# First mixture of a two-block transformer: experts taken by token count, 64 places for the three smallest, general path moved

## The chip, the cores and the metric

The kernel is one program on 1 core of one Trainium2 chip. The metric is the time of one execution on the device in microseconds (us). The three runs of the kernel before took 2213.13, 2216.81 and 2223.36 us, median 2216.81.

## The reference

A network of two blocks, 256 tokens of width 1024, all in float32. The part that matters here is the first mixture of experts, in the middle of the program:

```python
def moe_swiglu(h, router_w, router_b, w13, w2):
    logits = (h @ router_w).astype(jnp.float32) + router_b.astype(jnp.float32)
    top_val, top_idx = lax.top_k(logits, TOP_K_EXPERTS)
    top_w = jax.nn.softmax(top_val, axis=-1)
    gates = jnp.sum(jax.nn.one_hot(top_idx, N_EXPERTS, dtype=jnp.float32) * top_w[..., None], axis=-2)
    y = jnp.zeros_like(h)
    for e in range(N_EXPERTS):
        y = y + gates[..., e:e + 1] * swiglu(h, w13[e], w2[e])
    return y

def swiglu(h, w13, w2):
    a, b = jnp.split(h @ w13, 2, axis=-1)
    return (jax.nn.silu(a) * b) @ w2
```

`w13[e]` is 1024x7168 and `w2[e]` 3584x1024, so an expert has 44.04 MB of weights and all eight 352.3 MB. Only the tokens that chose an expert count for it. With the inputs of the reference the eight experts get 56, 70, 46, 49, 50, 90, 67 and 84 of the 512 choices.

## The kernel before

**Places.** An expert computes on CAP1 = 96 places: `select` makes a 0/1 matrix `q` (token by place), `fetch` brings the expert's tokens to the columns of `x` with matmuls, two experts at a time, `back` turns `q` round into `qT`, and `finish` adds the weighted results to the residual `R` with it. If one expert has more than 96 tokens, `overflow` (the general path, under a `tc.If` on a count that every engine loads into a register) does the rest; it stands ahead of the first `select`.

**Matmuls.** The weights move through the PE array; the tokens are the loaded side. A piece is 128 rows by 1024 columns of weights, 0.524 MB, and an expert has 84 of them, 56 of `w13` and 28 of `w2`. `unit` (L1212) splits the 96 places into three column groups of 32 that run side by side, each over three quarters of the piece's columns, 512 and then 256; a fourth group of 32 array columns takes the last quarter of the columns for all three. In total nine matmuls a piece; a float32 matmul shows as two records, so a piece shows as 18.

**Loop.** 33 steps `i`: step `i` does chunk `j = i % 4` of `w13` of expert `e = i // 4` (`first`), then the chunk of `w2` that belongs to step `i-1` (`down`), then `turn` transposes. Four steps make a position: position `e` runs expert `e`. At the last step `weighted`, `finish(7)` and `post(tb)` (residual and the two norms, for each half tb of the tokens) lead into block 2, whose first matmuls need `w_in`.

**Stream.** All weights of the program come through one list of loads, issued on SP's queue in program order by `Stream._load` (L136), each when the tile that it takes is free: a tile is free when PE has read it last. In the mixture the buffers are 9 `raw` tiles of 1 MB, `rh`/`rl` (1 MB) and, up to the mark `spl1` near the end, five pairs `wh`/`wl` (5 MB): 15 MB. Behind the mixture's weights the same list goes on with `w_in` of block 2, whose tiles are split into a high and a low part, `wh` on ACT (L149) and `wl` on DVE or, for the pieces named in `BEHIND`, on POOL (L153):

```python
        pool = (j, i) in self.pool
        after = self.behind if pool else self.after
        with self.k.tc.issue_after(after) if after is not None else ExitStack():
            (nc.gpsimd if pool else nc.vector).tensor_tensor(l, src, h.bitcast(F32), op=OP.subtract)
```

`FEW` limits how many of these splits may be made ahead of the end of the mixture.

Of the kernel before, what the change touches and what calls it, by code (L numbers as in the profile page):

```python
# [34 lines left out]
RAW2 = 7  # L35
FEW = 2
NB = 3
URGENT = 3000
TAIL = 2
CAP1 = 96  # L40
WIDE = (1024, 1024, 1024, 512)
# [5 lines left out]
HELD = 1  # L47
BEHIND = ((-1, 4), (0, 4))
POW = (1, 3, 5)
# [26 lines left out]
class Stream:  # L76


    def __init__(self, k, specs):
        self.k, self.specs = k, specs  # L80
        self.raw, self.sp = {}, {}
        self.pools = []
        self.cur = -1
        self.low = -1
        self.nd = 0

        self.pieces = []
        for j, (_, nk, n) in enumerate(specs):
            if nk:
                c = 2 if nk * n > 1024 else 1  # L90
                self.pieces += [(j, i, c) for i in range(c)]
        self.done = {}
        self.after = None
        self.hold = False
        self.limit = None
        self.behind = None
        self.pool = ()
        self.np = 0
        self.first = 0

# [23 lines left out]
    def _load(self, most=10 ** 6):  # L124
        while self.nd < min(len(self.specs), most):
            p = self._place(self.nd)
            if p is None:
                return
            j = self.nd
            m = len(p[4])  # L130
            ts = [p[0].tile([128, 2048 // m], F32, name=x) for x in p[4]]
            p[2].append(j)
            for view, src in self.specs[j][0]:
                nk = src.shape[1] // m
                for i, t in enumerate(ts):
                    self.k.nc.sync.dma_start(view(t, nk), src[:, nk * i:nk * i + nk])  # L136
            self.raw[j] = ts[0] if m == 1 else ts
            self.nd += 1
# [76 lines left out]
class K:  # L215
# [251 lines left out]
    def plan(self):  # L467
# [76 lines left out]
        ada(a1, 5, 1)  # L544
        self.marks["attn"] = len(sp)
        for i in range(33):
            if i < 32:
                e, j = divmod(i, 4)
                if i == 30:
                    self.marks["spl1"] = len(sp)  # L550
                nk = 2048 // WIDE[j]
                for kh in range(8 // nk):
                    for o in range(2):
                        sp.append(wspec(A["moe_w13"][0, e], 128 * nk * kh, nk, 3584 * o + 1024 * j, WIDE[j], False))
            if i:
                e, j = divmod(i - 1, 4)
                for kh in range(WIDE[j] // 256):
                    sp.append(wspec(A["moe_w2"][0, e], 1024 * j + 256 * kh, 2, 0, 1024, False))
        self.marks["moe"] = len(sp)
# [41 lines left out]

        self.S.pool = [(self.marks[x] + i // 2, i % 2) for x, n in zip(("moe", "moe2"), BEHIND) for i in range(*n)]
        self.S.add(self.raw, NB)

# [473 lines left out]

    def ranks(self, sel, n, bank, pos, mx):

# [7 lines left out]
        for tb in range(2):  # L1088
            nc.vector.scalar_tensor_tensor(pos[:, tb], ps[:, n * tb:n * tb + n], 1.0, sel[:, tb], op0=OP.add, op1=OP.mult)
            nc.vector.tensor_scalar(pos[:, tb], pos[:, tb], -1.0, None, op0=OP.add)  # L1090
        nc.vector.tensor_reduce(mx, ps[:, 2 * n:3 * n], axis=AX.X, op=OP.max)

# [28 lines left out]
    def moe_in(self, mp, rp, R):  # L1121

        nc, A, keep = self.nc, self.A, self.keep
        self.route_consts(mp, CAP1, 128, mp.tile([128, 2, 192], F32, name="q", bufs=1)[:, 0, 0:128])
        rw = mp.tile([128, 8, 8], F32, name="rw", bufs=1)
# [43 lines left out]
    def moe(self, mp, R, T, post):  # L1169
# [4 lines left out]
        mx = sm.tile([128, 1], F32, name="mx")  # L1174
        self.ranks(sel, 8, 7, pos, mx)
        w13 = A["moe_w13"][0]

        def select(p):

            q = mp.tile([128, 2, 192], F32R, name="q", bufs=1)  # L1180
            for i in range(2):
                for tb in range(2):
                    nc.vector.tensor_scalar(q[:, tb, 96 * i:96 * i + 96], self.slots[:, 0:96], pos[:, tb, 2 * p + i:2 * p + i + 1], None, op0=OP.is_equal)
            return q

        def fetch(q, x, k):

            ps = self.bank(7)
            for j in range(2):
                for i, (src, tb) in enumerate((src, tb) for src in (nh, nl) for tb in range(2)):  # L1190
                    self.mm(ps[:, 192 * j:192 * j + 192], src[:, tb, 128 * (k + j):128 * (k + j) + 128], q[:, tb], i == 0, i == 3)
            nc.scalar.activation(x[:, k:k + 2], ps[:, 0:384].rearrange("p (k n) -> p k n", k=2), AF.Copy)

# [11 lines left out]

        def room():
            a, b = tokens(), mp.tile([128, 768], F32, name="hT", bufs=1)
            a = a.rearrange("p k n -> p (k n)")
            return [a[:, 256 * k:256 * k + 256] for k in range(6)] + [b[:, 256 * k:256 * k + 256] for k in range(2)]

        self.overflow(mp, room, ("th", "tl"),
                      R, nh, nl, None, None, pos, gate, mx, self.G2, CAP1, 8, 3584,  # L1212
                      w13[:, :, 0:3584], w13[:, :, 3584:7168], A["moe_w2"][0], "o (k p) n -> p (o k) n")
        q = select(0)
        x = tokens()
        for k in range(0, 8, 2):
            fetch(q, x, k)

        y = None

        def unit(out, lhs, rhs, wide, first, last, shared=(True, True)):
# [5 lines left out]
            for c in range(0, 3 * n, m):  # L1227
# [4 lines left out]
                for r in range(c // n, (c + w) // n):  # L1232
                    self.mm(out(3, n * r, n), lhs(r, True), rhs[:, 3 * n:4 * n], start and n * r == c, stop and n * (r + 1) == c + w)

        def first(x, wide):
# [26 lines left out]

        def turn(h, wide):

            nb = 3 * wide // 512
            hT = mp.tile([128, 768], F32, name="hT", bufs=1)
# [27 lines left out]
        def weighted(e):  # L1294

            ys = []
            for h in range(2):
                yg = sm.tile([128, 512], F32, name="t512", bufs=3)
                n = 256 if h else 512
                nc.vector.tensor_tensor(yg[0:96, 0:n], y[h][0:96, 0:n], self.G2[0:96, 512 * h:512 * h + n], op=OP.mult)  # L1300
                if h:
                    for g in range(3):
                        t, c = (y[0], 256 * g) if g < 2 else (y[1], 0)
                        nc.vector.tensor_tensor(yg[32 * g:32 * g + 32, 256:512], t[96:128, c:c + 256], self.G2[96:128, 768:1024], op=OP.mult)
                if e < 7:
                    yh = mp.tile([128, 512], F32R, name="th")[0:96]
                    yl = mp.tile([128, 512], F32R, name="tl")[0:96]
                    self.split(yh, yl, yg[0:96])
                    ys.append((yh, yl))
                else:  # L1310
                    ys.append((yg[0:96],))
            return ys

        def finish(e, qT, ys):
            after = None
            for tb in range(2):
                pc = [self.bank(5 + h) for h in range(2)]
                for h in range(2):
                    for i, part in enumerate(ys[h]):
                        self.mm(pc[h], qT[:, tb] if e < 7 else qT[:, tb].bitcast(F32), part, i == 0, i == len(ys[h]) - 1)  # L1320
                with self.tc.issue_after(after) if after is not None else ExitStack():
                    for h in range(2):
                        c = slice(512 * h, 512 * h + 512)
                        nc.vector.scalar_tensor_tensor(R[:, tb, c], pc[h], gate[:, tb, e:e + 1], R[:, tb, c], op0=OP.mult, op1=OP.add)
                if e == 7:
# [4 lines left out]
        for i in range(33):  # L1330
            e, j = divmod(i, 4)
            if i < 32:
# [5 lines left out]
                if j == 0:  # L1338
                    xe = x[:, :, 96 * (e % 2):96 * (e % 2) + 96]
                    qT = back(q, e % 2)  # L1340
                h = first(xe, WIDE[j])
            if last is not None:
                if (i - 1) % 4 == 0:
                    y = [self.bank(3), self.bank(4)]
                down((i - 1) % 4, last)
                if j == 0:
# [3 lines left out]
            if i < 32:  # L1350
                last = turn(h, WIDE[j])
                if j == 0 and e:
                    finish(e - 1, qTl, ys)
                qTl = qT

                if e % 2 and e < 7:
# [5 lines left out]

    def overflow(self, mp, room, tags, R, nh, nl, a, b, pos, gate, mx, G, cap, n, F, wa_, wb_, w2_, order):

# [6 lines left out]
        with tc.If(most > cap):  # L1371
            go = mp.tile([128, 2, n], F32, name="go", bufs=1)
            nc.vector.scalar_tensor_tensor(go, pos, float(cap), gate, op0=OP.is_ge, op1=OP.mult)
            hT = room()
            for tb in range(2):
                for h in range(2):
                    ps = self.bank(4 + h)
                    for j in range(4):
# [578 lines left out]
    def moe2(self, mp, R, T, before, post):  # L1957
# [60 lines left out]
        with self.tc.issue_after(self.last_gs):  # L2018
            self.resid(R, ALPHA2, T["rows"])

        def room():
            t = mp.tile([128, 8, 256], F32, name="x1", bufs=1)
# [4 lines left out]
        for p in range(16):  # L2027
# [33 lines left out]
            if p == 4:  # L2061

                scatter(1, *last)
                pe.close()
                self.overflow(mp, room, ("yl", "yh"), R, nh, nl, a, b, pos, gate, mx, None, CAP2, 32, 256,
                              A["exp_gate_2"][0], A["exp_up_2"][0], A["exp_down_2"][0], "o (p k) n -> p (o k) n")
# [278 lines left out]
```

## Time and profile before

| what | value |
|---|---|
| median of three runs | 2216.81 us |
| time of the profiled execution | 2216.82 us |
| its span in the trace | 2215.1 us |
| first mixture, first `w13` matmul behind the first `qT` to the last matmul | 589.6 to 1538.8 us |
| start of positions 1 to 7 (ACT's copy of `qT`) | 696.5, 819.6, 936.1, 1059.1, 1174.7, 1296.5, 1413.0 us |

Time stamps are us from the start of the span. The profiled execution is the median run to 0.01 us. A group "x18" in a row of the timeline is 18 consecutive instructions of one shape; PEclk 1.00 is TensorE at its upper clock (2.4 GHz), 0.5 at its lower (1.2 GHz).

### The profile page before, as it was taken

What the parts mean: (1) busy time and instruction counts of PE and PEld (TensorE: products, weight loads), DVE (VectorE), ACT (ScalarE), POOL (GpSimd) and SP (SyncE); (2) the same over time, 40 slices, a digit from 0 to 9 for tenths busy, and PEclk for the clock granted to TensorE, in tenths of its full rate; (3) what the DMA queues carried; (4) which work ended last, traced back from release to release, by engine and by line L of the source; (5) the groups of instructions that cost most, each with busy time, mean ns of one, the idle gap of its engine ahead of it and who ended that gap; (6) DMA issues with size and microseconds to landing.
All of it is one profiled execution on the core that took longest, in us unless ns stands there. A gap on an engine that the chain in (4) does not pass through costs nothing. (4 is left out here: it accounts for less than half of the span.)

```text
span 2215.1 us, 45056 instructions
## 1 busy us (share of the span) xinstructions
PE 2105.9 (95%) x19755; PEld 1507.9 (68%) x19755; DVE 819.1 (37%) x1645; ACT 527.0 (24%) x917; POOL 134.4 (6%) x219
## 2 busy tenths in 40 slices
PE   7989999999799999999999999997899998999995
PEld 4756778767577677777686777765687887444444
DVE  4448776755200101010101010012596567433337
ACT  2244433653100000000000000001544334222123
POOL 2000000003400000000000000002010001000002
PEclk9999999999799999999999999999899999999997
DMA  9566895726699899999999999975343229699771
GB/s 351 186 228 232 310 322 182 266 98 234 252 401 388 340 370 372 390 353 387 334 395 360 392 360 378 391 273 184 106 146 98 86 73 337 254 378 371 287 289 57
DMA packets 248010, 620.87 MB, mean 280 GB/s; under 512 B 22719, under 2 KB 82065, under 8 KB 247808
## 3 DMA queue, kind: packets, MB, share of 16 engines
q1 hardware_dynamic: 241232, 613.60, 74.6%
q10 hardware_dynamic: 4784, 2.81, 0.5%
q8 instruction: 157, 2.57, 0.4%
q0 software_dynamic: 1792, 1.52, 0.4%
q14 instruction: 45, 0.37, 0.0%
HBM read 616.43 MB, written 1.44 MB: 279 GB/s over the span
## 5 line engine op out<-in xcount | busy, mean ns | idle before, releaser
L253 PE MATMUL b<-raw,x 128*32 128x256 f32 (+4 forms) x5632 | 486.7, 447 | 0.0
L253 PEld LDWEIGHTS b<-raw,x 128*32 128x32 f32 (+1 forms) x5632 | 297.4, 112 | 145.3 <-issue 56.0
L1260 DVE TENSOR_TENSOR h<-t,b 128x512 f32<-128x512 f32 (+2 forms) x56 | 30.9, 554 | 779.0 <-PE b L253 717.0
L253 PE MATMUL b<-raw,hT 128*32 128x256 f32 (+2 forms) x2712 | 247.2, 463 | 3.2 <-ACT hT L1272 3.2
L153 DVE TENSOR_TENSOR wl<-raw,wh 128x1024 fp32r<-128x1024 f32 (+1 forms) x167 | 203.7, 1225 | 100.1 <-ACT wh L149 96.8
L149 ACT ACTIVATE wh<-raw 128x1024 fp32r<-128x1024 f32 x175 | 183.3, 1053 | 207.3 <-PE b L253 184.2
L253 PEld LDWEIGHTS b<-raw,hT 128*32 128x32 f32 (+1 forms) x2712 | 155.5, 112 | 75.0 <-issue 30.4
L1259 ACT ACTIVATE t<-b 128x512 f32<-128x512 f32 (+2 forms) x56 | 27.5, 490 | 541.8 <-PE b L253 541.8
L253 PE MATMUL b<-wh,x 128*32 128x256 f32 (+4 forms) x1334 | 151.5, 449 | 0.8 <-DVEq L1371 0.8
L253 PE MATMUL b<-wl,x 128*32 128x256 f32 (+4 forms) x1334 | 150.5, 449 | 0.0
L253 PE MATMUL b<-wh,hTh 128*128 128x512 f32 x352 | 145.0, 414 | 5.2 <-ACT hTh L331 2.3
L253 PE MATMUL b<-wl,hTh 128*128 128x512 f32 x352 | 143.2, 407 | 0.0
L253 PE MATMUL b<-wh,hTl 128*128 128x512 f32 x352 | 142.5, 407 | 0.7 <-DVE hTl L347 0.7
L253 PE MATMUL b<-hTh,wh 128*128 128x256 f32 (+1 forms) x376 | 109.6, 291 | 0.7 <-ACT wh L149 0.7
L253 PE MATMUL b<-hTl,wh 128*128 128x256 f32 (+1 forms) x376 | 108.7, 289 | 0.0
L253 PE MATMUL b<-hTh,wl 128*128 128x256 f32 (+1 forms) x376 | 107.5, 287 | 0.2 <-DVE wl L153 0.2
L253 PEld LDWEIGHTS b<-wl,x 128*32 128x32 f32 (+1 forms) x1334 | 76.7, 111 | 32.3 <-issue 9.4
L253 PEld LDWEIGHTS b<-wh,x 128*32 128x32 f32 (+1 forms) x1334 | 74.1, 111 | 29.4 <-issue 5.2
L1272 ACT ACTIVATE hT<-b 128x512 f32<-128x512 f32 (+2 forms) x56 | 24.6, 484 | 261.4 <-PE b L1271 261.4
L253 PEld LDWEIGHTS b<-wh,hTh 128*128 128x128 f32 x352 | 68.4, 194 | 25.0 <-ACT hTh L346 3.2
L253 PEld LDWEIGHTS b<-wh,hTl 128*128 128x128 f32 x352 | 68.0, 193 | 17.7 <-DVE hTl L347 1.1
L253 PEld LDWEIGHTS b<-wl,hTh 128*128 128x128 f32 x352 | 68.3, 194 | 17.2 <-issue 1.9
(547 smaller groups left out, 3056.5 us busy)
## 6 DMA issues: line engine op xcount, KB each, us to landing
raw<-in_moe_w_dram SPq DMA_DIRECT2D x208, 1024.0 KB, 6.9
wh<-in_moe_w_dram SPq DMA_DIRECT2D x105, 512.0 KB, 6.6
wl<-in_moe_w_dram SPq DMA_DIRECT2D x105, 512.0 KB, 6.4
raw<-in_ada_w_dram SPq DMA_DIRECT2D x48, 1024.0 KB, 7.1
raw<-in_exp_down_dram SPq DMA_DIRECT2D x24, 1024.0 KB, 9.4
raw<-in_exp_gate_dram SPq DMA_DIRECT2D x47, 512.0 KB, 7.8
raw<-in_exp_up_dram SPq DMA_DIRECT2D x47, 512.0 KB, 9.0
raw<-in_ffn_w_dram SPq DMA_DIRECT2D x44, 512.0 KB, 7.1
```

The lines of the kernel that those rows point to most:

```text
L149: self.last_h = nc.scalar.activation(h, src, AF.Copy).ins
L153: (nc.gpsimd if pool else nc.vector).tensor_tensor(l, src, h.bitcast(F32), op=OP.subtract)
L253: self.last_mm = self.nc.tensor.matmul(out, lhsT, rhs, start=start, stop=stop).ins
L1259: nc.scalar.activation(sa, pa, AF.Silu)
L1260: nc.vector.tensor_tensor(h[:, c], sa, pb, op=OP.mult)
L1272: nc.scalar.activation(hT[:, 128 * o:128 * (o + m)], pt[:, 0:128 * m], AF.Copy)
```

## The change

Expert 0 stays first. The other seven are taken in falling order of their number of tokens, which the device finds out: `order()` makes a rank and a permutation `P` on DVE, some twenty operations on tiles of at most 128x49, and SP loads seven registers (`wi`). From position 1 on the source address of every weight load holds a register. `S.known` keeps the list of loads from going past expert 0 until the registers are known. Positions 0 to 4 have 96 places, positions 5 to 7 have 64: two column groups of 64, each over half the columns (`unit2`). With the reference's inputs the order is 56 (expert 0), 90, 84, 70, 67, 50, 49, 46, so the last three fit. Only expert 0's half of the tokens is fetched ahead of position 0, the other half in its four steps. `general` now stands after the first step of position 1. `BEHIND` and `FEW` give four `wl` splits of `w_in` from POOL to DVE.

```diff
-FEW = 2
+FEW = 4
-CAP1 = 96
+CAP1 = (96, 96, 96, 96, 96, 64, 64, 64)
-BEHIND = ((-1, 4), (0, 4))
+BEHIND = ((0, 0), (0, 4))
@@ Stream._load
-        while self.nd < min(len(self.specs), most):
+        while self.nd < min(len(self.specs), most, len(self.specs) if self.known is None else self.known):
...
+                src = src() if callable(src) else src
@@ plan
+        def chosen(w, s, r0, nk, c0, n):
+
+            if s == 0:
+                return wspec(w[0], r0, nk, c0, n, False)
+            view, _ = wspec(w[0], r0, nk, c0, n, False)[0][0]
+            src = lambda: w[bass.ds(self.expert[s], 1), r0:r0 + 128 * nk, c0:c0 + n].rearrange("o (k p) n -> p (o k) n", p=128)
+            return [(view, src)], 0, n
@@ the mixture
+        def order():
...
+            nc.vector.tensor_tensor(cmp, key[:, None, :].to_broadcast([128, 7, 7]), key[:, :, None].to_broadcast([128, 7, 7]), op=OP.is_lt)
...
+            _, self.expert[1:] = nc.values_load_multi_w_load_instructions(wi[0:1, 0:7], engines=[mybir.EngineType.SP], min_val=1, max_val=7)
+            self.S.known = None
...
-        self.overflow(mp, room, ("th", "tl"),
...
-        q = select(0)
+        q = select(0, (0,))
         x = tokens()
         for k in range(0, 8, 2):
-            fetch(q, x, k)
+            fetch(q, x, k, (0,))
+        spos, sgate, P = order()
+        select(0, (1,))
...
+        def unit2(out, lhs, rhs, wide, first, last, shared=(True, True)):
+
+            n = wide // 2
+            for g in range(2):
+                self.mm(out[64 * g:64 * g + 64, 0:n], lhs(g), rhs[:, n * g:n * g + n], first, last)
...
-                h = first(xe, WIDE[j])
+                h = (first if CAP1[e] == 96 else first2)(xe, WIDE[j])
...
-                down((i - 1) % 4, last)
+                (down if CAP1[(i - 1) // 4] == 96 else down2)((i - 1) % 4, last)
...
+                if e == 0:
+                    fetch(q, x, 2 * j, (1,))
+                if i == 4:
+                    general()
```

PE at the start of position 5. `b` are PSUM banks, `identr,q` is the turn of `q` into `qT`, `wh`, `wl` and `raw` hold weights, `x` the tokens. Before:

```order
L253 MATMUL b_9975<-identr,q 96x128 x2
L253 MATMUL b_9980<-wh,x 32x512 x3
L253 MATMUL b_9980<-wh,x 32x256 x2
L253 MATMUL b_9982<-wh,x 32x256 x4
L253 MATMUL b_9980<-wl,x 32x512 x3
L253 MATMUL b_9980<-wl,x 32x256 x2
L253 MATMUL b_9982<-wl,x 32x256 x4
```

And of the change:

```order
L256 MATMUL b_10128<-identr,q 96x128 x2
L256 MATMUL b_10133<-wh,x 64x512 x2
L256 MATMUL b_10133<-wl,x 64x512 x2
L256 MATMUL b_10134<-raw,x 64x512 x4
L256 MATMUL b_10133<-raw,x 64x512 x4
```

Nine matmuls a piece have become two.

SP, with the weight loads: the general path's place ahead of the mixture before, where it stands behind the loads that fit ahead of position 0.

```order
L136 DMA wh<-in_moe_w_dram 128x1024
L136 DMA wl<-in_moe_w_dram 128x1024
L1370 TENSOR_LOAD mi
L1371 COMPARE_AND_BRANCH
...
L1370 ISA x2
L136 DMA raw<-in_moe_w_dram 128x2x1024 x9
```

Of the change, at the same place (the load of the seven registers) and in position 1, where the branch now stands between loads:

```order
L139 DMA wl<-in_moe_w_dram 128x1024
L1219 TENSOR_LOAD wi
L1219 ISA x14
L139 DMA raw<-in_moe_w_dram 128x2x1024 x9
...
L139 ISA
L139 DMA raw<-in_moe_w_dram 128x2x1024
L1494 TENSOR_LOAD mi
L1495 COMPARE_AND_BRANCH
...
L1494 ISA x2
L139 ISA
L139 DMA raw<-in_moe_w_dram 128x2x1024
```

The branch has moved from a place ahead of the stream to one inside it, and behind it each load has an ISA instruction (the address) ahead of it.

DVE at the end of the mixture, `weighted` and `post(0)`. Before:

```order
L1300 TENSOR_TENSOR t_13060<-b_12480,G_81 96x512
L1300 TENSOR_TENSOR t_13062<-b_12481,G_81 96x256
L1304 TENSOR_TENSOR t_13062<-b_12480,G_81 32x256 x2
L1304 TENSOR_TENSOR t_13062<-b_12481,G_81 32x256
L1324 SCALAR_TENSOR_TENSOR R<-b_13067,gate,R 128x512
L316 BN_STATS bst<-R 128x6
L1324 SCALAR_TENSOR_TENSOR R<-b_13068,gate,R 128x512
L316 BN_STATS bst<-R 128x6
L289 BN_AGGR bmv<-bst 128x2
```

And of the change:

```order
L1416 TENSOR_TENSOR t_11354<-b_11149,G_81 64x512
L1416 TENSOR_TENSOR t_11356<-b_11149,G_81 64x512
L1443 SCALAR_TENSOR_TENSOR R<-b_11358,sorted,R 128x512
L156 TENSOR_TENSOR wl<-raw,wh 128x1024
L319 BN_STATS bst<-R 128x6
L156 TENSOR_TENSOR wl<-raw,wh 128x1024
L1443 SCALAR_TENSOR_TENSOR R<-b_11359,sorted,R 128x512
L156 TENSOR_TENSOR wl<-raw,wh 128x1024
L319 BN_STATS bst<-R 128x6
L156 TENSOR_TENSOR wl<-raw,wh 128x1024
L292 BN_AGGR bmv<-bst 128x2
```

Five operations of `weighted` have become two, and the four splits that POOL made stand between DVE's operations of the post.

## Rows read from the trace of the kernel before

**Rows 1.** The page, part 1: busy time of the engines, share, instructions.

```profile
PE 2105.9 (95%) x19755; PEld 1507.9 (68%) x19755; DVE 819.1 (37%) x1645; ACT 527.0 (24%) x917; POOL 134.4 (6%) x219
```

**Rows 2.** The page, part 2: 40 equal slices of 55.4 us.

```profile
PEclk9999999999799999999999999999899999999997
...
GB/s 351 186 228 232 310 322 182 266 98 234 252 401 388 340 370 372 390 353 387 334 395 360 392 360 378 391 273 184 106 146 98 86 73 337 254 378 371 287 289 57
```

**Rows 3.** Windows: stretch, length, PE, PEld, DVE, ACT, POOL busy (instructions), PEclk, DMA share, GB/s.

```profile
589.60:696.50 106.90, 106.51 (x1497) 79.45 (x1500) 4.17 (x9) 8.08 (x16) 0.00 (x0) 1.00 1.01 391
1174.70:1296.50 121.80, 120.59 (x1629) 89.57 (x1625) 10.84 (x22) 10.08 (x23) 0.00 (x0) 1.00 0.97 372
1296.50:1413.00 116.50, 116.50 (x1594) 85.44 (x1595) 10.38 (x18) 7.93 (x18) 0.00 (x0) 1.00 0.98 374
1413.00:1519.50 106.50, 106.50 (x1469) 78.91 (x1464) 10.38 (x18) 7.56 (x17) 0.00 (x0) 1.00 0.80 302
600.00:630.00 30.00, 29.61 (x410) 21.42 (x406) 1.11 (x2) 2.45 (x5) 0.00 (x0) 1.00 1.03 416
20.00:40.00 20.00, 13.86 (x87) 9.84 (x80) 11.29 (x16) 3.57 (x7) 4.91 (x3) 1.00 1.06 382
```

**Rows 4.** Waits of SP's queue, 550 to 1600: total us, times, longest.

```profile
SPq L136 <- PE b L253: 740.1, 445, 16.1
```

**Rows 5.** Timeline of PE in position 0: start, length, what.

```profile
650.25 1.51 PE L253 MATMUL b<-rh,x 128*32 128x512 f32 x18
651.54 1.51 PE L253 MATMUL b<-rl,x 128*32 128x512 f32 x18
```

**Rows 6.** Timeline of PE in the second mixture, groups of 64.

```profile
2001.29 0.59 PE L253 MATMUL b<-raw,x 128*64 128x512 f32 x1
2001.72 0.59 PE L253 MATMUL b<-raw,x 128*64 128x512 f32 x1
```

**Rows 7.** Timeline of ACT, start of position 5.

```profile
1174.74 0.37 ACT L1200 ACTIVATE qT<-b 96x256 fp32r<-96x256 f32 x1
```

**Rows 8.** Timeline of PE, end of the mixture and first matmul of block 2.

```profile
1531.95 6.88 PE L253 MATMUL b<-raw,hT 128*32 128x512 f32 x72 [3.22 <-ACT hT L1272]
...
1559.30 1.42 PE L253 MATMUL b<-wh,hTh 128*128 128x512 f32 x1
```

**Rows 9.** Timeline of PE ahead of position 0.

```profile
577.06 0.77 PE L253 MATMUL b<-q,hTh 128*128 128x192 f32 x2 [3.04 <-DVE q L1183]
...
589.23 0.38 PE L253 MATMUL b<-identr,q 128*96 128x128 f32 x2
```

**Rows 10.** Timeline of SP in the second mixture, loads around its general path.

```profile
1966.51 0.89 SPq L136 DMA_DIRECT2D raw<-in_exp_down_dram  x2
1972.92 0.36 SPq L136 DMA_DIRECT2D raw<-in_exp_gate_dram  x1
```

**Rows 11.** Windows around it, columns as in group 3.

```profile
1968.00:1970.00 2.00, 2.00 (x10) 0.57 (x6) 0.00 (x0) 0.00 (x0) 0.00 (x0) 1.00 0.87 218
1970.00:1972.00 2.00, 2.00 (x11) 1.46 (x11) 1.14 (x3) 0.45 (x2) 0.00 (x0) 1.00 0.94 320
1972.00:1974.00 2.00, 1.59 (x10) 1.14 (x8) 1.71 (x3) 0.32 (x1) 0.00 (x0) 1.00 1.04 422
```

**Rows 12.** Timeline of DVE behind the mixture.

```profile
1538.49 1.02 DVE L1300 TENSOR_TENSOR t<-b,G 96x512 f32<-96x512 f32 x2 [19.95 <-PE b L253]
1539.52 1.31 DVE L1304 TENSOR_TENSOR t<-b,G 32x256 f32<-32x256 f32 x3
...
1545.39 5.57 DVE L328 SCALAR_TENSOR_TENSOR R<-R,rstd,G 128x512 f32<-128x512 f32 x2
...
1563.48 1.41 DVE L328 SCALAR_TENSOR_TENSOR R<-R,rstd,G 128x512 f32<-128x512 f32 x2
...
1569.38 1.23 DVE L153 TENSOR_TENSOR wl<-raw,wh 128x1024 fp32r<-128x1024 f32 x1 [0.21 <-issue]
```

**Rows 13.** Timeline of POOL there.

```profile
1545.24 5.17 POOL L153 TENSOR_TENSOR wl<-raw,wh 128x1024 fp32r<-128x1024 f32 x2
```

**Rows 14.** Timeline of SP, first loads behind the mixture's.

```profile
1520.52 11.12 SPq L136 DMA_DIRECT2D raw<-in_w_in_dram  x4
```

## Prediction before the run

> **What bounds the kernel now.** I read the page first. TensorE is busy for 2105.9 of 2215.1 us [rows 1], but the slices show a second thing at its limit: from slice 11 to slice 25, which is the first mixture, the transfers move 334 to 401 GB/s [rows 2]. So I asked for windows of single positions of the mixture. In each, PE is busy for 99 to 100% of the time, at the full clock, and the DMA engines show a share of 0.97 to 1.01 while experts still have to be loaded [rows 3]. A share near 1 doesn't say which of the two is the bound, since it counts a packet that is held up as busy. The waits say it: SP's queue, which issues the loads, waits 740.1 us in 445 waits for PE to be done with a tile [rows 4], and no wait of PE between 550 and 1600 us ends on a load. So PE sets the pace and the loads follow.
>
> But they follow closely. A piece of 0.524 MB takes 1.29 us of PE (651.54 - 650.25 [rows 5]); that asks for 0.524/1.29 = 406 GB/s. Position 6 lasts 116.5 us for 84 pieces, 108.4 us of which are these matmuls and 8.1 us fetches, transposes and `finish`; over a position the demand is 374 GB/s, as the window shows. The question of this change is what the loads can give once PE asks for more.
>
> **64 places: what PE saves.** At 64 places a piece is two matmuls side by side. The second mixture has this shape in its trace: pairs start 0.43 us apart (2001.72 - 2001.29 [rows 6]), one record of a pair for each group of 64, and a float32 matmul is two records, so a piece costs 0.86 us. Saved are 0.43 us a piece, 3 x 84 x 0.43 = 108.4 us. Positions 5 to 7 last from 1174.7 [rows 7] to 1531.95 + 6.88 = 1538.8 [rows 8], 364.1 us; by PE alone they would take 255.7 us.
>
> **What the loads then cost.** In those windows come 121.8 x 372 + 116.5 x 374 + 106.5 x 302 GB/s = 45.3 + 43.6 + 32.2 = 121.0 MB [rows 3]; the other 11 of the three experts' 132.1 MB had landed before 1174.7 (the buffers hold 15 MB). For 255.7 us these 121.0 MB would need 473 GB/s, and no row has that. So the loads become the bound of positions 5 to 7, and the gain is cut by that. At what rate they run when nothing holds them back is the unknown price. From below: 351 GB/s, the mean of positions 5 to 7 themselves until the experts are loaded (121.0 MB in 344.8 us, 1174.7 to 1519.5), when PE held them back. From above: 416 GB/s in 30 us of position 0 [rows 3]. Between them lie 391 GB/s over the whole of position 0, the longest stretch with free room in the buffers, and 382 GB/s at 20 to 40 us, where PE is busy for only 69% at a DMA share of 1.06, but with other tiles. I take 400, between the two of position 0, since both are rates that PE's pace still held back in part: 121.0/0.400 = 302.5 us, and 2 us for the matmuls of the last tile, 305 us. Saved: 364.1 - 305 = 59 us. At 416 it is 71 us, at 385 48 us, at 351 17 us.
>
> The Trainium skill ("DMA: Bandwidth & Descriptors", Specifications) gives a core about 358 GB/s of the memory; by it the positions would take 338 + 2 us and the gain would be 24 us. The trace does not agree: 391 GB/s over 107 us [rows 3]. "HBM Reference", Specifications (TRN2), of the same skill says that a core streaming alone measures about 425; by that the gain would be 77 us, which no row here reaches for a whole position.
>
> **Start.** Ahead of position 0 the fetch of both halves runs from 577.06 to 589.23 [rows 9]; with half the columns I take 2 us off, the general path's branch at this place included. The other half's fetch comes in position 0: 4 x 8 matmuls of 96 columns, some 0.1 us each, +3.5 us since PE is full there. `order()` runs on DVE, which is busy for 4.17 us of position 0 [rows 3]; behind it SP's registers are late only if it took longer than the 44 MB of expert 0 last, some 100 us. It costs nothing; without that cover each of its twenty small operations would cost some 0.2 us.
>
> **The branch in the stream.** Every engine loads the count and branches after the first step of position 1. The second mixture has the same branch in full stream: SP issues nothing between 1966.51 + 0.89 and 1972.92 [rows 10], and the rate falls to 218 and 320 GB/s for 2 us each; PE loses 0.4 us [rows 11]. Queued behind SP's branch are loads; the 11 MB that stand ready are 25 us of PE's work. I take +1 us, from 0.4 to 5.
>
> **Register addresses.** Each load behind expert 0 has one more instruction on SP. A load of that queue is 0.36 us when issued back to back [rows 10], and a half-megabyte tile needs one per 1.31 us at 400 GB/s. I take nothing; it becomes a price where issue takes over 1.31 us.
>
> **End.** `weighted` takes 1.02 + 1.31 us in five operations [rows 12] and becomes two of the 0.5 us kind: -1.2 us. POOL's two splits take 5.17 us [rows 13], and DVE's two operations beside them 5.57 us where the same two take 1.41 later [rows 12]: -4.2 us once POOL is quiet. The four splits on DVE cost 1.23 us each [rows 12], +4.9. Sum -0.5 us. The first `w_in` loads were issued at 1520.52, 18 us before the last matmul [rows 14]; now they come directly behind the last expert's load. A megabyte at 400 GB/s is 2.6 us, so the first three are there 8 us after it, and block 2's first matmul came 20.5 us after the mixture's last (1559.30 - 1538.8 [rows 8]). Hidden, and if it weren't, some 3 us.
>
> **Sum.** 2216.8 (profiled execution, equal to the median) - 59 - 2 + 3.5 + 1 - 0.5 = 2159.8; I say 2159 us.
>
> **Rivals.**
> (1) Loads bound positions 5 to 7 at 385 to 416 GB/s: 2172 to 2148 us. Chance 0.70.
> (2) The loads are slower than that when they run alone, 351 to 385 GB/s. For it speaks that the slices of the mixture reach 401 only once and lie at 334 to 395 elsewhere [rows 2]. Then 2172 to 2202 us. Chance 0.19.
> (3) PE bounds them all the same: 2216.8 - 108 + 2 = 2111 us. It needs 473 GB/s against 416. Chance 0.01.
> (4) Slower: the loads with a register address, from position 1 on, are slow in themselves (each has its address worked out on SP, and nothing before has it for such tiles). Behind expert 0 come 308.3 MB, of which 11 have landed at 698 us; at 353 GB/s the other 297 MB end where they ended before, 842 us later at 1540. At 320 GB/s they take 929 us and the program 2304 us. It decides from 353 GB/s down. Against it: SP has 0.9 us to spare for each tile. Chance 0.04.
> (5) Slower: TensorE falls to 1.2 GHz because it now waits for loads. A position of 64 places is 72.2 + 8.1 = 80.3 us of PE at the full clock, 161 us at half; three would last 482 us against 364, and the program 2335 us. It decides where more than two thirds of the positions' time runs at half clock. Against it: at 20 to 40 us PE is busy for 69% and PEclk is 1.00 [rows 3]; positions 5 to 7 would be busy for 3 x 80.3/305 = 79%. Chance 0.02. The Trainium skill ("TensorE: Matmul & The Clock Gate", HAM oscillation) tells of a kernel whose clock fell at each tile since its matmuls were shorter than the wait for the next; the window at 20 to 40 us doesn't show it.
> (6) The gain is lost in something small (a branch that drains 10 us, a run of late tiles), or the counts are not the ones that I worked out and the general path runs: 0.04, 2200 us or more, for the most part within 11 us of no change.
>
> **How the numbers follow.** The predicted time is that of (1). About 0.5% (11 us) is what a measurement of this kernel tells from no change. The range leaves out (3) to (6), 0.11, and the slow end of (2), 0.06: from 2144 (416 GB/s less the 4 us by which runs lie under the median) to 2190 (about 362 GB/s). Case (1) alone is 2147 to 2172. Faster by over 0.5%: (1), (2) and (3), which end at 2202 us at the latest, and 0.01 of (6), 0.91; same: the rest of (6), 0.03; slower: (4) and (5), 0.06.
>
> **What would show it.** In the changed kernel PE should wait for loads in positions 5 to 7, busy for 75 to 80%, at PEclk 1.00; SP should wait for PE hardly at all there; the windows should show about 400 GB/s; positions 5 to 7 should take 305 us together, positions 0 to 4 what they took. Around the branch in position 1 the loads should dip for about 5 us with PE undisturbed. Behind the mixture the two stretched operations of DVE should take 1.4 us, followed or preceded by four splits of 1.23. The forecast is wrong if positions 1 to 4 get longer (register addresses), if PEclk drops, or if the rate without PE's brake is not near 400.

## The result, and the profile after

The changed kernel took 2151.86 to 2159.84 us in four runs, median 2157.57; the kernel before 2213.13 to 2223.36, median 2217.78. The ratio is 0.9724, with a 95% interval of 0.9694 to 0.9754: 60 us, or 2.8%, faster. The prediction was 2159 us.

First the page of the changed kernel, its slices (54.0 us each), against [rows 2]. Positions 5 to 7 lie in slices 21 to 27, counted from 0.

```profile
PEclk9999999999699999999999999997999798999997
...
GB/s 352 199 234 225 315 317 201 262 103 212 216 385 386 284 407 353 387 395 340 369 359 395 413 417 413 416 411 214 137 145 100 40 101 337 289 379 371 285 278 56
```

The rate stands at 411 to 417 GB/s in slices 22 to 26, which lie wholly inside them, where it swung between 334 and 401 over the mixture before. Windows of the same kernel, with the columns of [rows 3]: positions 0 and 1, positions 5 to 7 together, the stretch from the mixture's last matmul to block 2's first, and the rest of the program.

```profile
585.80:697.50 111.70, 111.70 (x1529) 81.91 (x1532) 3.89 (x8) 9.42 (x21) 0.00 (x0) 0.99 1.00 380
697.50:824.00 126.50, 124.12 (x1627) 90.59 (x1628) 11.19 (x22) 10.01 (x21) 0.00 (x0) 0.97 0.91 353
1180.60:1476.40 295.80, 260.33 (x1278) 90.34 (x1274) 25.55 (x42) 19.70 (x38) 1.27 (x3) 1.00 1.03 414
...
1476.40:1497.70 21.30, 8.03 (x18) 3.22 (x16) 17.73 (x30) 8.70 (x12) 1.66 (x3) 0.63 0.42 138
1497.70:2158.10 660.40, 616.33 (x3747) 414.27 (x3746) 363.48 (x814) 207.56 (x372) 49.20 (x96) 0.93 0.58 206
```

Positions 5 to 7 take 295.8 us, 68.3 less than the 364.1 of before, and PE is now the engine with time to spare: busy for 260.3 us, at PEclk 1.00. Its waits in that stretch (total us, times, longest) and, in a second fence, those of SP's queue:

```profile
PE b L256 <- DMA raw<-in_moe_w_dram: 21.1, 28, 1.7
```

```profile
SPq L139 <- PE b L256: 94.7, 72, 5.1
SPq L139 <- DMA raw<-in_moe_w_dram: 44.8, 29, 3.4
```

PE waits for loads, which it did nowhere in the mixture before. The first of these waits comes at 1321 us, 140 us into the stretch: until then PE lives in part on what had been loaded ahead. SP, which waited 266.3 us for PE in these positions before (1174 to 1520 us), still waits 94.7 us for it, and now for its earlier transfers too.

### The profile page after: what moved, and what is told of

Read it like the earlier page. It is cut to its first block, busy times and chain, and to the rows that moved or that the text cites. A ratio compares the mean times of both kernels' runs of the same rounds, so it can differ in the third digit from the quotient of the medians.

```text
span 2158.1 us, 38724 instructions
## 1 busy us (share of the span) xinstructions
PE 2021.9 (94%) x16190; PEld 1345.7 (62%) x16190; DVE 817.4 (38%) x1657; ACT 520.2 (24%) x902; POOL 124.2 (6%) x215
## 5 line engine op out<-in xcount | busy, mean ns | idle before, releaser
L256 PE MATMUL b<-raw,x 128*32 128x256 f32 (+5 forms) x4100 | 443.5, 466 | 17.6 <-DMA raw<-in_moe_w_dram 15.3
L256 PEld LDWEIGHTS b<-raw,x 128*32 128x32 f32 (+1 forms) x4100 | 230.2, 116 | 188.0 <-issue 92.9
L156 DVE TENSOR_TENSOR wl<-raw,wh 128x1024 fp32r<-128x1024 f32 x171 | 208.8, 1227 | 97.0 <-ACT wh L152 95.3
L256 PE MATMUL b<-raw,hT 128*32 128x256 f32 (+2 forms) x1928 | 222.7, 485 | 5.9 <-DMA raw<-in_moe_w_dram 5.8
L1373 DVE TENSOR_TENSOR h<-t,b 128x512 f32<-128x512 f32 (+2 forms) x35 | 19.4, 555 | 486.9 <-PE b L256 445.9
L256 PEld LDWEIGHTS b<-raw,hT 128*32 128x32 f32 (+1 forms) x1928 | 112.5, 116 | 94.3 <-issue 54.7
L256 PE MATMUL b<-wh,x 128*32 128x256 f32 (+4 forms) x984 | 132.1, 464 | 0.8 <-DMA wh<-in_moe_w_dram 0.7
L256 PE MATMUL b<-wl,x 128*32 128x256 f32 (+4 forms) x984 | 131.2, 463 | 1.1 <-DMA wl<-in_moe_w_dram 0.5
L1385 ACT ACTIVATE hT<-b 128x512 f32<-128x512 f32 (+2 forms) x47 | 21.9, 499 | 275.2 <-PE b L1384 176.9
L256 PEld LDWEIGHTS b<-wl,x 128*32 128x32 f32 (+1 forms) x984 | 60.9, 114 | 40.6 <-issue 19.4
L256 PEld LDWEIGHTS b<-wh,x 128*32 128x32 f32 (+1 forms) x984 | 58.9, 114 | 36.0 <-issue 13.5
```

The source lines that it names most:

```text
L256: self.last_mm = self.nc.tensor.matmul(out, lhsT, rhs, start=start, stop=stop).ins
L1373: nc.vector.tensor_tensor(h[:, c], sa, pb, op=OP.mult)
L1385: nc.scalar.activation(hT[:, 128 * o:128 * (o + m)], pt[:, 0:128 * m], AF.Copy)
```

## The experiments

All are edits of the changed kernel, or of an edit named in their text; ratios are against the kernel before, which ran beside each.

**96 places throughout.** The order, the registers, the branch and the splits stay.

```diff
-CAP1 = (96, 96, 96, 96, 96, 64, 64, 64)
+CAP1 = (96,) * 8
```

> The changed kernel with 96 places in all eight positions; order by count, register addresses, the moved branch and the splits on DVE stay. My account (the gain is that of the 64 places alone, and the rest of the change costs some us): positions 5 to 7 take 364 us again, PE there busy for 99% and never behind a load, the rate 370 to 375 GB/s; the program takes 2216.8 + 6 (the start of position 5 is 6 us later in the changed kernel than before) = 2222 us, up to 2228 if the 24 us at the lower clock in block 2 of the changed kernel show here too. Rival (taking the experts by count, or the addresses in registers, is worth something by itself): under 2205 us.

2220.05 us, ratio 1.0017 (0.9993 to 1.0041): no gain is left. Positions 5 to 7 in its windows:

```profile
1179.80:1546.60 366.80, 362.47 (x4875) 263.72 (x4866) 36.77 (x62) 30.98 (x61) 1.42 (x4) 0.99 0.91 342
```

PE is busy for 99% again and the rate is that of before. The gain is that of the 64 places; the rest of the change is worth nothing or some us to the bad.

One thing is better here than in both other kernels: from the mixture's last matmul to block 2's first it takes 16.3 us (1546.6 to 1562.9), against 20.5 before and 21.3 in the changed kernel. The loads run ahead of PE, `w_in` is issued 19.6 us before the mixture's end, and DVE makes the four splits before that end, so that nothing of them is left in the stretch:

```profile
1533.24 2.36 DVE L156 TENSOR_TENSOR wl<-raw,wh 128x1024 fp32r<-128x1024 f32 x2 [8.21 <-ACT wh L152]
1537.04 2.36 DVE L156 TENSOR_TENSOR wl<-raw,wh 128x1024 fp32r<-128x1024 f32 x2 [1.43 <-ACT wh L152]
```

In the changed kernel the same four stand between DVE's operations at 1479.05 to 1485.51 us, 1.2 us each.

**Half the matmul columns in positions 5 to 7**, with the same loads.

```diff
-                self.mm(out[64 * g:64 * g + 64, 0:n], lhs(g), rhs[:, n * g:n * g + n], first, last)
+                m = n if first or last else n // 2
+                self.mm(out[64 * g:64 * g + 64, 0:m], lhs(g), rhs[:, n * g:n * g + m], first, last)
```

> The changed kernel, whose matmuls in positions 5 to 7 take only half the columns of all pieces but the first and the last of a sum (this part of the result is left out); the loads are the same. Matmuls of a position of 64 places fall from 72 to some 43 us. My account (the loads bound these positions): 295 to 297 us from the start of position 5 to the mixture's end as in the changed kernel, 412 to 418 GB/s, also if PEclk falls there. Rival 1 (PE, with its waits for single tiles, still sets part of the pace): under 285 us and a higher rate. Rival 2 (with less PE work the clock falls and PE becomes the bound): over 300 us.

One execution; its result leaves out part of the sums. Positions 5 to 7:

```profile
1177.60:1473.90 296.30, 212.11 (x1278) 94.36 (x1274) 25.66 (x42) 19.85 (x38) 1.42 (x4) 0.87 1.03 414
```

The same 296 us at the same 414 GB/s, with some 50 us less of PE's work and with TensorE at its lower clock for a quarter of the time (PEclk 0.87). Neither PE's work nor its clock sets these positions. The loads do, at the same rate. Which part of their path holds them there (the memory, the DMA engines, the queue, the number of tiles in flight), no run here tells apart.

**Addresses written into the program** in place of registers, no wait of the list at expert 0.

```diff
-            src = lambda: w[bass.ds(self.expert[s], 1), r0:r0 + 128 * nk, c0:c0 + n].rearrange("o (k p) n -> p (o k) n", p=128)
-            return [(view, src)], 0, n
+            return wspec(w[(0, 5, 7, 1, 6, 4, 3, 2)[s]], r0, nk, c0, n, False)
```

> The changed kernel with the order of the experts written into the program for these inputs: no registers, no wait of the list of loads at expert 0, one instruction less on SP ahead of each load; the tiny sorting operations on DVE stay. My account (a register address costs nothing that shows, since SP has some 0.9 us to spare per load): the program within 3 us of the changed kernel's 2157.6 us, positions 5 to 7 at 294 to 298 us and 412 to 418 GB/s. Rival (the addresses in registers slow the loads): positions 5 to 7 under 290 us, a rate above 420 GB/s, the program under 2150 us.

2152.6 us, 0.9706 (0.9682 to 0.9731); positions 5 to 7 take 295.5 us at 412 GB/s, positions 2 to 4 what they took. The program is 5 us under the changed kernel, where I expected it within 3; the intervals overlap, and block 2 alone is 5.3 us shorter in its profile (below). No price of register addresses shows.

**No general path**, and **the branch at position 5**, where the loads are the bound.

```diff
-                if i == 4:
-                    general()
```

> The changed kernel without the general path and its branch in position 1 (these inputs never take it). My account (the drained queues around the branch cost PE about 1 us and lengthen the stretch at the lower clock that follows the fetches): position 1 goes from 126.5 to 123 to 125 us, all else as in the changed kernel, the program 2154 to 2157 us. Rival 1 (the branch costs nothing, position 1 is longer for another reason): 126 to 127 us. Rival 2 (the branch is what delays positions 2 to 4 too): the start of position 5 comes 5 us earlier or more.

```diff
-                if i == 4:
+                if i == 20:
                     general()
```

> The changed kernel with the branch behind the first step of position 5 instead of position 1: nothing is loaded ahead there, the loads are the bound. My account (PE stands some 10 us for SP, as in the run with four small experts, but PE has 33 us to spare in positions 5 to 7, and the loads stop for a few us at most): positions 5 to 7 take 296 to 302 us against 295.8, position 1 stays at 123 to 124 us, the program 2150 to 2162 us. Rival (PE's stop, or the loads' stop behind it, is paid in full): 305 us or more.

Without the branch: 2150.86 us, 0.9704 (0.9679 to 0.9728), under the 2154 to 2157 that I expected, position 1 at 123.4 us. That agrees with the first account on its face and yet doesn't support it: five kernels with the branch in its place have 121.7 to 124.2 us there, at PEclk 1.00. The 126.5 of the changed kernel's profile is that execution's, at PEclk 0.97. With the branch at position 5, position 1 takes 122.0. So the times bound the branch at position 1 only to some 2 us; in the changed kernel's waits, those of PE that end on it or stand right behind it come to about 1 us. The loads pause longer with it: in the changed kernel they move 7 to 8 GB/s from 730 to 740 us, where without the branch the pause is 5 us long (31 GB/s from 730 to 735, then 265).

At position 5 the branch costs 6.9 us, over the 296 to 302 us that I expected:

```profile
1179.80:1482.50 302.70, 261.25 (x1278) 91.22 (x1274) 25.56 (x42) 19.83 (x38) 1.27 (x3) 0.98 1.01 403
1200.00:1220.00 20.00, 11.64 (x44) 5.00 (x46) 4.84 (x8) 1.26 (x3) 0.00 (x0) 0.74 0.70 261
```

PE stands still for 8 us of the 20 about the branch; the loads lose 20 x (414 - 261) GB/s = 3.1 MB, 7.4 us at 414 GB/s, and that is what is paid. The rival was right in kind (the loads' stop is paid in full), though not at its 305 us. Two things in my account were wrong. PE's longest wait there, 6.5 us, ends on PE's own branch and not on SP's; SP then waits 9.2 us for PE to free a tile. And loads had run ahead: PE's first wait for one comes at 1323 us. What was loaded ahead keeps PE from waiting, but in a stretch that the loads bound it doesn't give back the time in which they stop. The program: 2160.12 us, 0.9752 (0.9711 to 0.9792).

**Both halves of the first tokens fetched ahead of position 0**, with the sorting ahead of them.

```diff
-        q = select(0, (0,))
+        spos, sgate, P = order()
+        q = select(0)
         x = tokens()
         for k in range(0, 8, 2):
-            fetch(q, x, k, (0,))
-        spos, sgate, P = order()
-        select(0, (1,))
+            fetch(q, x, k)
...
-                if e == 0:
-                    fetch(q, x, 2 * j, (1,))
```

> The changed kernel with both halves of the first tokens fetched ahead of position 0, which needs the sorting of the experts ahead of them too. My account (the 32 matmuls of the second half are what makes position 0 longer, 111.7 against 106.9 us before): position 0 takes 106 to 108 us again, it starts 3 to 8 us later than in the changed kernel (fetch and the some twenty operations of the sorting on DVE), the program 2155 to 2162 us. Rival (position 0 is longer because the loads start later or the clock is low at its start): position 0 stays at 111 us or more.

Position 0 takes 106.9 us as before: the 32 matmuls of the second half are its 4.8 us. It starts 3.3 us later, but 2.6 of these had passed before the edit has any effect (the matmul `sel,q` of the routing, ahead of the fetch, starts at 570.11 against 567.49 us); its own price is 0.7 us. 2150.75 us, 0.9711 (0.9682 to 0.9739), under the 2155 to 2162 that I expected, with an interval that overlaps the changed kernel's. The price is that of whole matmuls. In the changed kernel, with half the columns, ahead of position 0:

```profile
572.07 0.63 PE L256 MATMUL b<-q,hTl 128*128 128x96 f32 x2
572.50 0.62 PE L256 MATMUL b<-q,hTh 128*128 128x96 f32 x2
```

and with all of them in this kernel:

```profile
577.46 0.63 PE L256 MATMUL b<-q,hTl 128*128 128x192 f32 x2
577.88 0.63 PE L256 MATMUL b<-q,hTh 128*128 128x192 f32 x2
```

Both 0.42 to 0.43 us apart, at PEclk 0.50. At PEclk 1.00 both are 0.22 us apart (640.19 and 640.41 us in the changed kernel, 586.90 and 587.12 in this one). So 96 columns cost what 192 do, and fetching in two parts doubles the fetch.

**The splits on POOL again.**

```diff
-FEW = 4
+FEW = 2
-BEHIND = ((0, 0), (0, 4))
+BEHIND = ((-1, 4), (0, 4))
```

> The changed kernel with the four wl splits of w_in on POOL again and FEW at 2, as before. My account (what DVE gains by POOL's silence it pays in splits): from the last matmul of the mixture to the first of block 2 20 to 22 us against 21.3 in the changed kernel, DVE's two operations that took 5.57 us before take over 4 us again, the program within 3 us of 2157.6 us unless the stretch at the lower clock in block 2 goes. Rival 1 (the splits on DVE are what puts block 2 into that stretch): PEclk 1.00 between the 205th and 240th us behind the mixture's end, the program 5 us shorter. Rival 2 (with loads as the bound, w_in comes later and POOL's splits would be late): 25 us or more.

2155.93 us, 0.972 (0.9697 to 0.9743). From the mixture's end to block 2's first matmul 24.0 us against 21.3, over the 20 to 22 that I expected. DVE in this kernel:

```profile
1483.80 3.50 DVE L330 SCALAR_TENSOR_TENSOR R<-R,bmv,xh 128x512 f32<-128x512 f32 x2
1487.78 5.58 DVE L331 SCALAR_TENSOR_TENSOR R<-R,rstd,G 128x512 f32<-128x512 f32 x2 [0.49 <-POOL rstd L270]
```

Both pairs take 1.41 us in the changed kernel. In the kernel before, POOL had made two of its splits before the mixture's end (1526.57 us) and made two behind it; here `w_in` comes later, all four come behind the end (from 1481.10 us), and they stretch two pairs instead of one. So the move to DVE is worth 2.7 us behind 64 places. Neither rival held: block 2 kept its stretch at the lower clock (PEclk 0.68 from 1683.6 to 1718.6 us, where the first rival wanted 1.00), and 24.0 us is under the second's 25.

**The small experts spread.** If 96 places are bound by PE and 64 by the loads, each can cover the other through the 15 MB of buffers. `RANK` says which rank in the order by count each of positions 1 to 7 takes.

```diff
-CAP1 = (96, 96, 96, 96, 96, 64, 64, 64)
+CAP1 = (96, 64, 96, 96, 64, 96, 96, 64)
+RANK = (4, 0, 1, 5, 2, 3, 6)
...
+            at = sm.tile([128, 7], F32, name="at", bufs=1)
+            for s in range(7):
+                nc.vector.memset(at[:, s:s + 1], float(RANK[s]))
-            nc.vector.tensor_tensor(P, rank[:, None, :].to_broadcast([128, 7, 7]), n[:, :, None].to_broadcast([128, 7, 7]), op=OP.is_equal)
+            nc.vector.tensor_tensor(P, rank[:, None, :].to_broadcast([128, 7, 7]), at[:, :, None].to_broadcast([128, 7, 7]), op=OP.is_equal)
```

> The changed kernel with the three small experts at positions 1, 4 and 7 and the others between them in falling order (places 96, 64, 96, 96, 64, 96, 96, 64). My account (96 places are bound by PE, 64 by the loads, and what is loaded ahead in the buffers, some 10 MB or 25 us of loads, evens it out over two positions of 96 and one of 64): a position of 64 places takes 80 to 88 us instead of 99, those of 96 stay at 115 to 125; the mixture 112 + 3 x 82 + 4 x 120 = 838 us instead of 890.6, PE waits for loads under 10 us in all, the program about 2106 us (2100 to 2118). Rival 1 (what is loaded ahead is used up at once, or is not built up again at 370 GB/s): 64 places take 95 to 99 us in each place, the program 2145 us or more. Rival 2 (the rate in positions of 96 is at its own limit near 375 and cannot rise, so the buffers are empty after the first small one): position 1 fast, positions 4 and 7 near 99 us, the program about 2135 us.

2127.28 us, 0.9596 (0.9574 to 0.9617): 30 us better than the change, where I expected 50. The mixture:

```profile
592.10:1454.10 862.00, 853.73 (x9230) 502.16 (x9227) 73.39 (x131) 66.37 (x135) 1.13 (x2) 1.00 1.01 396
```

The mechanism held: PE is busy for 99%, and none of its waits ends on a load. The size was off: I gave a position of 64 places 82 us, from the position of [rows 3] with 8.1 us of other work, but every second position fetches tokens too and has 14.7 (123.1 us in position 1, less 108.4); positions 1 and 7 here take 89 us. Summed over whole positions, the mixture before (949.2 us) less 108.4 and plus 4.8 is 846 us. Of the other 16 us, 13 lie in positions 4 to 6 (1034.5 to 1365.1 us, 330.6 against 353.9 - 36.1 = 317.8 before). There single matmuls of the fetch and of `finish` stand between those of the 64 places; that this is what costs them isn't shown.

**The same with both halves fetched ahead.** The two edits together.

> The small experts at positions 1, 4 and 7 and both halves of the first tokens fetched ahead of position 0, the two edits together. My account (position 0 loses the 4.8 us of the second fetch, the start gains 3.3 us; the mixture with the small experts spread is bound by PE, so nothing of that is hidden by loads): the mixture 857 us instead of 862, the program 1 to 3 us under the run with the small experts spread, 2122 to 2130 us. Rival (with PE as the bound nowhere, it is the loads that end the mixture): no change of its end, the mixture 859 us or more, PE's waits for loads over 10 us.

2126.47 us, 0.9592 (0.9573 to 0.9612), the mixture 857.9 us: 4.1 us less, position 0 alone 4.7 (106.9 for 111.6); the program's difference can't be told from none.

**Expert 0 at 64 places too**, four small experts spread, an edit of the run before it with both halves fetched ahead, and **the same with the branch at position 3**.

```diff
-CAP1 = (96, 64, 96, 96, 64, 96, 96, 64)
-RANK = (4, 0, 1, 5, 2, 3, 6)
+CAP1 = (64, 96, 96, 64, 96, 64, 96, 64)
+RANK = (0, 1, 4, 2, 5, 3, 6)
```

> As the run before it here, with expert 0 (56 tokens) at 64 places too and the small ones at positions 0, 3, 5 and 7. PE has 36 us less to do, 826 us with what the run with three spread ones measured; the loads that are still to come at the start of position 0, about 339 MB, need 339/0.414 = 819 us and 2 for the last tile. My account (the mixture ends by the later of the two): 826 to 835 us, PE's waits for loads 5 to 20 us, a rate of 400 to 414 GB/s over the mixture, the program 2090 to 2102 us. Rival 1 (where both engines have nothing to spare, their pauses add up): 840 us or more, the program over 2105 us. Rival 2 (the loads have more to give than 414 GB/s when PE never stops them): under 820 us.

```diff
-                if i == 4:
+                if i == 12:
                     general()
```

> The run with four small experts spread, with the general path's branch behind the first step of position 3 instead of position 1. There PE stood for 14 us behind the branch (the longest wait 11.2 us, for SP, which comes to the branch only when all loads ahead of it are issued; at position 1 what had been loaded ahead was used up by then, since position 0 has 64 places). My account (ahead of position 3 two positions of 96 places have let the loads run ahead again, and SP is through the branch before PE needs what is behind it): PE's wait for SP under 3 us, the mixture 828 to 836 us instead of 843.9, the program 2097 to 2104 us. Rival (PE stands as long at the new place, the wait belongs to the branch itself): PE's wait for SP over 8 us, the mixture 840 us or more.

Branch at position 1: 2111.69 us, 0.9522 (0.9501 to 0.9543), the mixture 843.9 us: over what I expected and inside the first rival's range (840 us or more, the program over 2105). PE's waits for loads come to 3.8 us, under the 5 to 20 that I expected. Its longest wait is another; here are that group of waits and the window around it:

```profile
PE b L257 <- SPq L1496: 14.1, 5, 11.2
```

```profile
695.00:705.00 10.00, 0.34 (x1) 0.00 (x0) 1.03 (x2) 0.00 (x0) 0.00 (x0) 0.50 1.02 417
```

PE stands still while the loads run at 417 GB/s: SP reaches its own branch only at 704.6 us, behind loads that it issues as earlier transfers end, and PE's next matmul starts at 706.5, released by SP from behind the branch. At position 3 that wait is gone (PE waits 0.3 us at the branch), and the mixture takes 835.2 us at 409 GB/s, 8.7 us less:

```profile
589.00:1424.20 835.20, 817.33 (x8009) 452.19 (x8007) 71.21 (x125) 61.54 (x123) 1.13 (x2) 0.99 1.02 409
```

2107.58 us, 0.9503 (0.9462 to 0.9544), the best of the study, over the 2097 to 2104 expected. In its profiled execution, the slowest of the four (2113.08 us; the fastest took 2100.81), block 2 took 665.8 us against 654.4 in that of the run with the branch at position 1; what it took in the other three isn't known. It beats the changed kernel by 50 us and the kernel before by 109. For other inputs it holds as well as the change does as long as expert 0 has at most 64 tokens; else the general path runs.

## Why the prediction was right

**The main term** (positions 5 to 7, loads as the bound) was right in kind and 9 us too small: 295.8 us for 305, since the loads run at 414 GB/s and not at 400. The row to choose was the 416 GB/s of 30 us in position 0 [rows 3], which I had taken for the upper end; the rate of all of position 0 was still held back by PE. 121.0 MB at 414 GB/s and the 2 us of the last tile make 294 us. The half-column kernel shows that PE doesn't set the rate, and four other kernels with 64 places at the end have 295.5 to 296.4 us there. By the rule of the Trainium skill ("DMA: Bandwidth & Descriptors", Specifications: about 358 GB/s for a core) it would have been 340 us; 414 GB/s over 296 us disagrees. The Trainium skill's "HBM Reference", Specifications (TRN2), puts a core that streams alone at about 425, which is 3% over what is measured here.

**The price of the rest** was too small by about as much, and the errors cancelled: that the sum came within 2 us of the median is luck. In the profiled execution, against the one before: start of position 0 -3.9 us (-2 forecast), position 0 +4.8 (+3.5), position 1 +3.4 (+1), positions 2 to 4 +1.4 (0), positions 5 to 7 -68.3 (-59), end of the mixture to block 2 +0.8 (-0.5), block 2 +4.6 (0); in sum -57.2 us, the spans' difference -57.0.

- Start: the step was wrong. Half the columns save nothing, and the -3.9 us isn't the change's: the routing's matmul `sel,q` already stood at 567.49 us against 572.56, 5.1 us earlier. From it to position 0 the changed kernel takes 18.3 us, as do seven others with the same start, against 17.1 before: +1.2 us where -2 was forecast.
- Position 0: right; the term was mis-sized at 0.1 us a matmul, 4.8/32 = 0.15 us measured.
- Branch: right in size at position 1, about 1 us of PE's waits; the loads' pause was 10 us and not 5. The rest of the +3.4 goes with the lower clock of that execution (PEclk 0.97 over the position; 0.77 from 725 to 730 us, 0.55 from 730 to 735). The loads' stop is hidden there because PE is the bound; elsewhere the branch costs 6.9 us at position 5 and 8.7 us of the mixture with four small experts. For the latter the prediction named the loads behind SP's branch but not that PE itself can be released from behind it.
- Registers: right; nothing.
- End: the three terms were right one by one (`weighted` in 1.41 us, the pairs of DVE at 1.41, splits of 1.2 each), with a sum of nothing until DVE is done, 20.6 to 20.7 us behind the mixture's end in both kernels. The 0.8 us are for the most part a matter of where the record of block 2's first matmul starts: its second starts 21.7 us behind the mixture's end before and 21.9 now. `w_in` was issued at 1464.4 us, 12 us ahead of that end, and no wait of block 2's first matmul ends on it. But "hidden" is only half right. With loads as the bound it comes too late for the splits to be made ahead; with 96 places throughout they were, and DVE was done 16.6 us behind the end, 4 us sooner.
- Block 2: no step spoke of it. The changed kernel shows TensorE at 1.2 GHz in the first of these windows, 192 to 212 us behind block 2's first matmul, where the kernel before shows 2.4 GHz at 188 to 208 us (the second fence):

```profile
1690.00:1710.00 20.00, 20.00 (x130) 16.33 (x130) 6.01 (x15) 2.59 (x5) 0.00 (x0) 0.50 0.00 1
```

```profile
1747.00:1767.00 20.00, 19.77 (x217) 15.99 (x216) 12.35 (x27) 6.21 (x12) 0.00 (x0) 1.00 0.17 54
```

Nothing ties that stretch to the change: block 2 from its first matmul takes 651.3 to 665.8 us over the kernels here, which don't differ in it, and 661.2 with 96 places throughout. What starts it stays open.

Two of the signs came out otherwise. PE was busy for 88% and not 75 to 80: the sign took 80.3 us a position from the lightest one, while the prediction's own 255.7 us for the three give 86% of 295.8. And SP still waited for PE, 94.7 us in 72 waits; in the half-column kernel it did so for 76.7 us at the same rate, so these waits don't set the pace.

The rivals: that the loads alone run at 351 to 385 GB/s fails by the 414 measured. That PE would fall to half clock and become the bound fails twice, since PEclk was 1.00 in positions 5 to 7 of the change, and in the half-column kernel it fell to 0.87 at no cost. That loads with register addresses are slow fails by the 414 GB/s they reach.

## What to carry to other kernels

Where PE asks for nearly all that the loads can give (406 of 414 GB/s here), cutting PE's work in one stretch buys only down to the loads; take the ceiling from a short window in which the rate is highest, not from the mean of a stretch that PE holds back. Work bound by loads and work bound by PE belong next to each other, within the reach of the buffers: the same three experts are worth 60 us at the end and 90 us when spread. What is loaded late has a second price: work that follows it, here the splits, can no longer be done ahead (4 us here). A branch that every engine takes is nearly free in a stretch that PE bounds and where loads have run ahead (about 1 us). Where the loads are the bound, the time in which they stop behind it is paid (6.9 us), and where SP comes to it late, PE stands for it (8.7 us of the mixture).

## What the runs showed of the hardware that was not expected

A matmul of the fetch with 96 columns, with a 128x128 tile loaded for each, took as long as one of 192: 0.42 to 0.43 us for two at 1.2 GHz, 0.22 us for two at 2.4 GHz. The rate of the loads over positions 5 to 7 stayed within 412 to 414 GB/s in six kernels, while PE was busy for 212 to 263 us; only the branch inside these positions lowered it (403). And TensorE ran at its lower clock for 20 us in a stretch where the profile shows it busy for all of them.
